# A 3x3 convolution: one half-image store cut into a 112-partition piece and four 4-partition pieces

## The chip, the cores and the metric

The kernel runs on one core of a Trainium2 chip. The metric is the device time of one execution in microseconds (us), the median of several runs. A core has five engines that run their own instruction queues side by side: TensorE (PE, matrix products), VectorE (DVE), ScalarE (ACT), GpSimd (POOL) and SyncE (SP, which here only issues transfers and waits). Transfers between the chip's main memory (HBM) and the core's own memory (SBUF, 128 partitions) are done by 16 DMA engines. A transfer is cut into packets, each of which is handled by one DMA engine; here a packet is one partition's contiguous row. When all DMA engines that take part have reported, the transfer has landed.

## What is computed

A 3x3 convolution with padding 1 of 16 images of 64 channels and 64x64 pixels to 128 channels. Nine tenths of the weights are zero, but the kernel treats them as dense.

```python
for b in range(batch):            # 16
    for co in range(c_out):       # 128
        for ci in range(c_in):    # 64
            for kh in range(k):
                for kw in range(k):
                    output[b, co] += weight[co, ci, kh, kw] * x_pad[b, ci, kh:kh+h, kw:kw+w]
```

Input and output are float32; an output image is 128 channels by 4096 pixels, 2 MB, and the whole output is 33.55 MB.

## The kernel before

Images go in pairs: eight pairs, p = 0 to 7. The 64 channels of the pair's two images lie side by side on the 128 partitions of a tile `xs[p]` in bfloat16. POOL issues the loads of all pairs at the start (L63, L67), with the conversion on the way; SP issues the weights (L60) and half of the first pair (L62). The weights are converted, transposed on PE, and summed and subtracted into five sets of taps (L103 to L118).

For each pair, four blocks of 16 rows are worked off in order (the loop at L175). Nearly all go through `twos` (L151): POOL adds neighbouring rows of x (L154), PE multiplies the sums (L157) and ACT copies that product to SBUF (L161); PE then multiplies the even and the odd rows' remaining terms, and DVE adds the copied product and writes the result into the pair's output tile `o[n]` (L168), n = 0 and 1 for the two images. The very first block uses `direct` (L144) instead. All products come from L135. The scheduler is manual: the order of instructions on each engine is the order in which the code is written.

An output tile `o` has 128 partitions (the output channels) of 64 x 64 float32, 16 KB each. The pool of these tiles has seven buffers (L47); the first tile of it holds the half pair that SP loads (L61), the other sixteen are the output images. When a pair is done, SP issues one store for each of its two images (L188): 128 partitions of 16 KB each. For the last pair SP issues two stores per image, of 32 rows each, so 8 KB per partition (L185). SP's queue holds, in order, the two loads, 14 stores of L188, four stores of L185, and the waits for their landing at the end of the program (L214).

The stores of p = 0 to 7 are issued as soon as DVE has written the pair. Those of the sixth pair (p = 5) are the eleventh and twelfth of L188's stores.

Of the kernel before, what the change touches and what calls it, by code (L numbers as in the profile page):

```python
# [27 lines left out]
def kernel(  # L28
# [6 lines left out]
    nc = tc.nc  # L35

    B, C_IN, H, W = x.shape
    C_OUT, _, KH, KW = weight.shape
    assert (B, C_IN, H, W) == (16, 64, 64, 64) and (C_OUT, KH, KW) == (128, 3, 3)
    NP = B // 2  # L40
# [103 lines left out]
    def direct(p, o, r0, rows):  # L144
        ps = product(
            [(xs[p], G1, r0, 1), (xs[p], G0, r0 - 1, 1), (xs[p], G2, r0 + 1, 1)], rows
        )
        nc.scalar.copy(out=o[0][:, r0 : r0 + rows, :], in_=ps[0])  # L148
        nc.vector.tensor_copy(out=o[1][:, r0 : r0 + rows, :], in_=ps[1])  # L149

    def twos(p, o, r0):  # L151
        t0 = r0 // 2
        s = s_pool.tile([128, 8, W], BF16, name="s")
        nc.gpsimd.tensor_tensor(  # L154
            out=s, in0=xs[p][:, r0 : r0 + 16 : 2, :], in1=xs[p][:, r0 + 1 : r0 + 16 : 2, :], op=ADD
        )
        shared = product([(s, G1, 0, 1)], 8)  # L157
        pc = []
        for n in range(2):
            c = p_pool.tile([128, 8, W], FP32, name="pc")  # L160
            nc.scalar.copy(out=c, in_=shared[n])  # L161
            pc.append(c)
        even = [(xs[p], G21, r0 + 1, 2), (xs[p], G0, r0 - 1, 2)]
        odd = [(xs[p], G01, r0, 2), (xs[p], G2, r0 + 2, 2)]
        for first, terms in ((r0, even), (r0 + 1, odd)):
            ps = product(terms, 8)
            for n in range(2):
                nc.vector.tensor_tensor(  # L168
                    out=o[n][:, first : r0 + 16 : 2, :], in0=ps[n], in1=pc[n], op=ADD
                )  # L170

    for p in range(NP):
        o = [o_pool.tile([C_OUT, H, W], FP32, name="o") for _ in range(2)]
        last = p == NP - 1
        for blk in range(4):  # L175
            r0 = 16 * blk
            if BLOCKS[p][blk] == "T":
                twos(p, o, r0)
            else:
                for r, rows in ((r0, 8), (r0 + 8, 8)):  # L180
                    direct(p, o, r, rows)
            if last and blk % 2 == 1:
                for n in range(2):
                    rows = slice(r0 - 16, r0 + 16)
                    nc.sync.dma_start(out=out[2 * p + n][:, rows, :], in_=o[n][:, rows, :])  # L185
        if not last:
            for n in range(2):
                nc.sync.dma_start(out=out[2 * p + n], in_=o[n])  # L188


# [28 lines left out]
```

## Time and profile before

| what | value |
|---|---|
| time, median of 6 runs | 127.7 us (127.58 to 127.92) |
| time of the profiled execution | 127.75 us |
| its span, from the first to the last instruction | 125.9 us |
| PE busy | 108.9 us, 86% of the span |
| DVE busy | 82.3 us, 65% |
| ACT, POOL busy | 39.0 and 40.8 us |
| granted TensorE clock, mean | 0.95 |
| HBM read and written | 17.07 and 33.55 MB, 402 GB/s over the span |
| stores of a whole image (L188) | 14, median 18.5 us from issue to landing |
| stores of half an image (L185) | 4, median 10.9 us |

The times of the groups of instructions come from one profiled execution; the median comes from runs beside it. In the profile the 16 DMA engines are shown together: a share of 1.00 means that all of them were at work all the time. The packet records of the trace give each packet's start, duration and size, but not the number of the DMA engine; the landing records give the time of each of the sixteen reports of a transfer. Where the text speaks of one engine's packets, they were put together from these records: each packet of an engine begins a few nanoseconds before the end of the one before it.

### The profile page before, as it was taken

The page shows a single profiled execution, that of the slowest core. Times are in us where ns is not written, and L with a number is a line of the kernel's source. Part 1 is how long each engine was busy: PE and PEld are TensorE (multiplying, and loading weights), DVE is VectorE, ACT ScalarE, POOL GpSimd, SP SyncE. Part 2 cuts the span into 40 slices and gives each one's busy share as a digit, 9 for nine tenths or more (in the row PEclk, how much of TensorE's full clock was granted, in tenths as well). Part 3 has the DMA queues.
Part 4 walks back from the last instruction along what each step waited for, and adds up shares of the span by engine and source line. Part 5 has one row for each costly group of instructions (what it writes and reads, how often), then busy time and mean ns, then how long its engine had stood idle before and what let it go on. Part 6 is the DMA issues. An engine that isn't in the chain of part 4 may idle for free.

```text
span 125.9 us, 2486 instructions
## 1 busy us (share of the span) xinstructions
PE 108.9 (86%) x1002; PEld 59.1 (47%) x1002; DVE 82.3 (65%) x135; ACT 39.0 (31%) x71; POOL 40.8 (32%) x45
## 2 busy tenths in 40 slices
PE   6569999999999999999999999999999999960000
PEld 6334555555555555555555555555555555520000
DVE  0352477877787778777787778777877787771000
ACT  4541533333333333333333333333333333320000
POOL 6937333333333333333333333333333320000000
PEclk9977999999999999999999999999999999999555
DMA  4999999999999999999999999999999999999980
GB/s 115 352 223 221 213 219 213 208 182 338 302 315 333 333 299 333 320 312 346 427 437 422 416 432 443 432 424 411 427 443 427 437 417 416 432 414 414 424 346 18
DMA packets 4044, 42.93 MB, mean 341 GB/s; under 512 B 448, under 2 KB 448, under 8 KB 704
## 3 DMA queue, kind: packets, MB, share of 16 engines
q1 hardware_dynamic: 2880, 34.90, 66.0%
q0 software_dynamic: 1152, 7.86, 30.8%
q8 instruction: 8, 0.13, 0.4%
q14 instruction: 4, 0.03, 0.1%
HBM read 17.07 MB, written 33.55 MB: 402 GB/s over the span
## 4 chain that ended last, share of the span: by engine, by line
PE 82%; DMA 4%; DVE 1%; issue 1%; DVEq 0%; SPq 0%
PE ps L135 82%; DMA o<-in_x_dram 4%; DVE o L168 1%; DVEq L214 0%; DVE x L87 0%; SPq L60 0%; DVEq L168 0%
## 5 line engine op out<-in xcount | busy, mean ns | idle before, releaser
L168 DVE TENSOR_TENSOR o<-ps,pc 128x512 f32<-128x512 f32 x124 | 77.8, 686 | 22.1 <-PE ps L135 19.8
L135 PE MATMUL ps<-x,wT 64*128 64x504 bf16 (+3 forms) x780 | 90.5, 379 | 2.0 <-DVE x L87 2.0
L135 PEld LDWEIGHTS <-wT 64*128 64x128 bf16 x966 | 55.8, 95 | 50.9 <-issue 3.6
L154 POOL TENSOR_TENSOR s<-x 128x512 bf16<-128x512 bf16 x31 | 35.7, 1152 | 59.6 <-PE ps L135 43.2
L161 ACT COPY pc<-ps 128x512 f32<-128x512 f32 x62 | 33.3, 589 | 64.0 <-issue 61.8
L135 PE MATMUL ps<-s,wT 64*128 64x512 bf16 (+1 forms) x186 | 25.7, 377 | 0.0
L74 PE MATMUL ps<-idle_rhs 128*128 128x128 bf16 x27 | 3.1, 313 | 1.0 <-DVE idle_rhs L71 1.0
L149 DVE COPY o<-ps 128x512 f32<-128x512 f32 x2 | 1.4, 692 | 3.7 <-PE ps L135 3.7
L67 POOL DMA_DIRECT2D x<-in_x_dram x7 | 3.7, 556 | 0.0
L74 PEld LDWEIGHTS <-idle_rhs 128*128 128x128 bf16 x27 | 2.8, 148 | 1.0 <-DVE idle_rhs L71 1.0
L91 DVE CAST w_bf<-w_sb 128x192 bf16<-128x192 f32 (+1 forms) x4 | 1.1, 347 | 2.9 <-DMA w_sb<-in_weight_dram 2.9
L148 ACT COPY o<-ps 128x512 f32<-128x512 f32 x2 | 1.2, 586 | 4.1 <-PE ps L135 4.1
L87 ACT CAST x<-o 128x576 bf16<-128x576 f32 (+1 forms) x2 | 1.5, 802 | 0.9 <-DMA o<-in_x_dram 0.9
L87 DVE CAST x<-o 128x576 bf16<-128x576 f32 x1 | 0.5, 460 | 1.8 <-DMA o<-in_x_dram 1.8
L91 ACT ACT_TABLE_LOAD x1 | 1.3, 1283 | 0.7 <-PEq L203 0.7
L91 ACT CAST w_bf<-w_sb 128x64 bf16<-128x64 f32 (+1 forms) x2 | 0.7, 415 | 1.8 <-DMA w_sb<-in_weight_dram 1.8
L97 PE MATMUL ps<-ident,w_bf 128*128 128x128 bf16 x9 | 0.9, 222 | 0.4 <-DVE w_bf L91 0.4
L101 DVE TENSOR_TENSOR wT<-ps,wT 128x384 bf16<-128x384 f32 x2 | 1.0, 548 | 0.0
L63 POOL DMA_DIRECT2D x<-in_x_dram x1 | 0.7, 696 | 0.8 <-POOLq L203 0.8
L97 PEld LDWEIGHTS <-w_bf 128*128 128x128 bf16 x9 | 0.5, 97 | 0.9 <-DVE w_bf L91 0.9
L71 DVE MEMSET idle_rhs<- 128x64 uint32 x1 | 0.1, 112 | 0.8 <-PEq L203 0.8
L112 DVE CAST wT<-ps 128x384 bf16<-128x384 f32 x1 | 0.6, 551 | 0.0
(8 smaller groups left out, 1.9 us busy)
## 6 DMA issues: line engine op xcount, KB each, us to landing
out_dram<-o SPq DMA_DIRECT2D x14, 2048.0 KB, 18.5
x<-in_x_dram POOLq DMA_DIRECT2D x7, 1024.0 KB, 27.3
out_dram<-o SPq DMA_DIRECT2D x4, 1024.0 KB, 10.9
o<-in_x_dram SPq DMA_DIRECT2D x1, 1024.0 KB, 5.6
x<-in_x_dram POOLq DMA_DIRECT2D x1, 512.0 KB, 7.7
w_sb<-in_weight_dram SPq DMA_DIRECT2D x1, 288.0 KB, 3.1
```

The lines of the kernel that those rows point to most:

```text
L67: nc.gpsimd.dma_start(out=xs[p], in_=pair(p))
L74: nc.tensor.matmul(idle_ps, idle_rhs, idle_rhs, start=True, stop=True)
L87: copy(out=xs[0][:, a:b, :], in_=x_head[:, a:b, :])
L91: copy(out=w_bf4[:, g, a:b, :], in_=w_v[:, k : k + b - a, :])
L97: nc.tensor.matmul(wps[:, j, :], src, ident, start=True, stop=True)
L101: nc.vector.tensor_tensor(out=wT[:, g], in0=wps, in1=wT[:, G1], op=SUB)
L135: nc.tensor.matmul(ps[n][:, lo:hi, c_lo:c_hi], tap(g, kw, n), src[q, a:b:step, c_lo + kw - 1 : c_hi + kw - 1], start=(i == 0), stop=(i == ...
L148: nc.scalar.copy(out=o[0][:, r0 : r0 + rows, :], in_=ps[0])
L149: nc.vector.tensor_copy(out=o[1][:, r0 : r0 + rows, :], in_=ps[1])
L154: nc.gpsimd.tensor_tensor(out=s, in0=xs[p][:, r0 : r0 + 16 : 2, :], in1=xs[p][:, r0 + 1 : r0 + 16 : 2, :], op=ADD)
L161: nc.scalar.copy(out=c, in_=shared[n])
L168: nc.vector.tensor_tensor(out=o[n][:, first : r0 + 16 : 2, :], in0=ps[n], in1=pc[n], op=ADD)
```

## The change

The store of image 0 of the sixth pair (p = NP - 3 = 5, n = 0) is issued in six pieces. Its first 32 rows are one store of 128 partitions with 8 KB each. Its last 32 rows are one store of partitions 0 to 111, and four stores of 4 partitions each (112 to 115, 116 to 119, 120 to 123, 124 to 127), again with 8 KB per partition. All other stores are as before, and so is every instruction of the other engines. By the change's own description, the 112 partitions give every DMA engine seven packets where it had eight, and each store of 4 partitions gives one packet to each of the DMA engines 0 to 3, so that these carry three packets of 8 KB more and all others one less.

```diff
         if not last:
             for n in range(2):
-                nc.sync.dma_start(out=out[2 * p + n], in_=o[n])
+                pieces = [(0, 128, 0, H)]
+                if (p, n) == (NP - 3, 0):
+
+                    pieces = [(0, 128, 0, H // 2), (0, 112, H // 2, H)]
+                    pieces += [(c, c + 4, H // 2, H) for c in range(112, 128, 4)]
+                for c0, c1, a, b in pieces:
+                    nc.sync.dma_start(
+                        out=out[2 * p + n][c0:c1, a:b, :], in_=o[n][c0:c1, a:b, :]
+                    )
```

## The prediction

> **What bounds the kernel now.** I read the page's slices first, then the chain that ended last, the waits of SP, a table of windows over the end, and last the trace's packet and landing records (start and duration of each DMA packet; time at which each of a store's sixteen engines reported). The slices:
>
> ```profile
> PE   6569999999999999999999999999999999960000
> ...
> DMA  4999999999999999999999999999999999999980
> ```
>
> PE is full until about 112 us. The DMA engines are full too, and go on alone for the last four slices. The chain of work, in order of time, follows only engines, and ends with DVE:
>
> ```profile
> 7.31 103.77 PE ps L135 x954
> ...
> 111.75 0.68 DVE o L168
> 112.43 0.60 DVEq L214
> 113.03 0.60 DVE o L168
> ```
>
> The span is 125.9 us, so 12.3 us lie behind that last addition. The waits of SP's queue say what they are: at the program's end (L214) SP waits for the last stores.
>
> ```profile
> SPq L188 <- DVE o L168: 94.1, 14, 21.8
> SPq L185 <- DVE o L168: 10.5, 4, 5.3
> SPq L214 <- DMA out_dram<-o: 9.8, 4, 2.6
> ```
>
> The table of windows shows how the transfers end (the last two columns are the share of the 16 DMA engines that is busy, and GB/s):
>
> ```profile
> 62.00:90.00 28.00, 28.00 (x266) 15.04 (x264) 21.90 (x36) 9.43 (x18) 10.24 (x9) 1.00 1.01 427
> ...
> 120.00:121.00 1.00, 0.00 (x0) 0.00 (x0) 0.00 (x0) 0.00 (x0) 0.00 (x0) 0.50 0.99 418
> 121.00:122.00 1.00, 0.00 (x0) 0.00 (x0) 0.00 (x0) 0.00 (x0) 0.00 (x0) 0.50 0.76 320
> 122.00:123.00 1.00, 0.00 (x0) 0.00 (x0) 0.00 (x0) 0.00 (x0) 0.00 (x0) 0.50 0.39 164
> 123.00:124.00 1.00, 0.00 (x0) 0.00 (x0) 0.00 (x0) 0.00 (x0) 0.00 (x0) 0.50 0.10 41
> ```
>
> From 62 us on the stores have a backlog and all engines stay full; at the end they run out one by one between 121 and 124.3 us. The last store's landing records are 121.46, 121.60, 121.79, 122.13, 122.16, 122.24, 122.39, 122.81, 122.96, 122.98, 123.01, 123.25, 123.32, 123.39, 123.79 and **124.74**. The latest engine sets the end: 1.14 us later the span is over. So the time is that of the slowest DMA engine, and a packet moved from one engine to another counts at full price from the changed store on.
>
> **The change, part by part.** The sum is made against the profiled execution: span 125.9 us, 1.85 us around it, 127.75 us. The median of six is 127.7.
>
> *Packets.* Packets of 16 KB (a full store's row) last 611 ns in 1190 of the 1279 records from 62 to 111 us, and overlap by 4: 607 each. A full store is eight of them per engine and a 6 ns report, 4.862 us, which is the distance of landings. Packets of 8 KB (half a row) last 309 ns, 305.7 each; the last four stores land 2.452 us apart. The changed store then takes on engines 4 to 15 2.452 + 7 x 0.3057 + 0.006 = 4.598 us, that is **0.264 us less**. On engines 0 to 3 four packets with reports of their own are added, 4 x 0.312 = 1.247, so 5.845 us, **0.983 us more**.
>
> *At the end.* If the latest engine is not among 0 to 3, it lands at 124.74 - 0.264 = 124.48. Engines 0 to 3 stay below that if they landed by 123.49 before, as 14 of 16 did. The records have no engine numbers. Four engines drawn from the other fifteen have their latest at four fifths, the 12th: 123.25, which becomes 124.23. Counting alone gives 127.75 - 0.26 = 127.49.
>
> The latest engine is a special one: its 16 KB packets last 634 to 662 ns while the compute engines run, and those of the rest 611. The Trainium skill ("DMA: Bandwidth & Descriptors", Latency and other measured facts) says that engines 7 and 15 are usually the slower ones. This trace has one slow engine and no numbers; by that rule it lies outside 0 to 3, and counting gives -0.26 and not +0.98 us.
>
> *Who reads what.* In each store of before, the same 128 rows are dealt to the 16 engines in the same way, and one engine's packets do not lengthen another's: 611 ns nearly everywhere. 112 rows in sevens can't keep that deal. The seven packets of an engine fall on rows that in the full stores belong to its neighbours, which are at work at the same time; the four pieces give engines 0 to 3 sixteen rows whose usual engines are, at that moment, reading others of their own rows. Eleven packets of engines 0 to 3, and up to seven of every other, may share a way into SBUF. No row of this case shows two engines on one way. From below the price is nothing (a gain is excluded: an engine that reads its own rows is at its best, 611). From above, the nearest rows are load packets between 25.5 and 28 us, when the first stores come in beside the loads: 0.8 to 1.25 us and once 1.42, against 0.625 alone, so about a doubling. The window's rate fell with it:
>
> ```profile
> 25.50:28.00 2.50, 2.50 (x27) 1.28 (x24) 1.77 (x4) 1.07 (x2) 1.15 (x1) 1.00 0.96 138
> ```
>
> I take a doubling where an engine surely meets another one (the four pieces, whose rows' own engines never pause) and half of the seven: 7.5 x 0.306 = 2.29 us on engines 0 to 3, 3.5 x 0.306 = 1.07 us on the others. Ends: 0 and 11 x 0.306 = 3.36 us. Engines 0 to 3 then land at 123.25 + 0.983 + 2.29 = 126.52, the slow engine at 124.48 + 1.07 = 125.55. The end moves by 126.52 - 124.74 = 1.78: 127.75 + 1.78 = **129.5 us**. With all eleven doubled, at the 14th landing: 123.39 + 0.983 + 3.36 = 127.73, 130.7 us.
>
> Why I take it although the loads speak against it: from 10 to 22 us an engine needs 606 ns for a load packet that reads 16 KB but writes only 8 KB to SBUF, so the engine's own rate is the limit there, and the way into SBUF may have room. But 16 stores' streams of 27.0 GB/s without a trace of scatter look like sixteen separate ways. The Trainium skill ("SBUF — State Buffer", Door 1: The DMA port swizzle) speaks against this change: eight partitions hang on one port, and four partitions alone reach 27.6 GB/s. By it a port's bytes do not change when another engine fetches them, nothing can be gained, and two engines on a port get half each, an estimate of 0.61 us a packet; no run here shows it.
>
> *Issuing.* SP issues six DMAs where it issued one. Two issues take 0.93 us:
>
> ```profile
> 87.45 0.93 SPq L188 DMA_DIRECT2D out_dram<-o  x2
> ```
>
> At 0.60 each, the store queued behind them on SP (the pair's second image) is issued at 91.05 and not 88.05. The first engine reports the changed store at 97.06 and only then needs the next: 6 us of cover, so nothing. If a piece took 1.05 us, as the slowest issue (L185) does, 93.3 would still do. Nobody else is on SP until pair 6 at 100.25. The o tile of this store is the twelfth of 17 in seven buffers, so no later tile waits for it. PE, DVE, ACT and POOL have the same instructions in the same order.
>
> **The rivals.**
> - *No sharing* (the other side): counting alone holds, 127.49 us, 0.21% faster. For it: the load packets above. Against it: the even 611. It decides as long as engines 0 to 3 lose less than 124.74 - 124.23 = 0.5 us over eleven packets, 46 ns each, and the slow engine less than 0.26 us over seven, 38 ns each.
> - *The slow engine is one of 0 to 3*, without sharing: 124.74 + 0.98, 128.7 us. One in four by blind drawing; against it, in the rush of 25.5 to 28 us this engine's packets lengthen later than those of at least six others, so it is hardly one of the first four to be served.
> - *The pieces don't spread*: all sixteen packets on one engine, 16 x 0.312 - 0.264 = +4.7 us; at a middle landing of 122.9 that is 127.6, so 130.6 us.
>
> **How the numbers follow.** Sharing at a price that shows: 0.52, forecast 129.5, its own range 128.0 to 130.8. No sharing: 0.36; the expected gain of 0.21% lies at the limit of 0.2%, which is about what a measurement of this kernel can tell from no change, so I split it 0.23 faster and 0.13 the same. Light sharing that eats just the gain: 0.04, the same. Slow engine among 0 to 3: 0.05. No spread: 0.03. Faster 0.23, same 0.17, slower 0.60. The range reaches from 127.4 (counting, less a tenth) to 131.0 (all eleven doubled, and some scatter); sharing by more than two engines at once, left out, has about one in ten.
>
> **What would show it.** In the packet records after about 92 us: 112 + 16 packets of 8 KB with 309 ns say no sharing, with 400 to 700 sharing. Sharing would also press the rate below 420 GB/s for some microseconds in the windows between 92 and 100. At the end, the window of 123 to 124 us is emptier if counting holds and busier, with landings past 125, if not. A PE or DVE wait that is new would prove me wrong on the cover, and a landing of the pair's second image that is late by itself on the issuing. The forecast is wrong if two engines can read one group of rows at full speed.

## The result, and the profile after

The changed kernel takes **128.6 us** (median of 21 runs, 127.61 to 129.51); the kernel before, beside it, 127.72 us (42 runs, 127.28 to 128.8). The ratio is 1.0057, with a 95% interval of 1.0037 to 1.0077: slower, by 0.7 us and not by 1.8. Ratios leave out runs more than 1.5% above the fastest of their kernel, and need not be those of the medians beside them. The 21 runs fall in two groups with nothing between 127.90 and 128.29: 8 runs at 127.61 to 127.90, which is the time before, and 13 at 128.29 to 129.51. The profiled execution belongs to the upper group: 129.27 us, span 127.5.

The first two fences are the busy rows and the chain of the changed kernel. PE's chain starts 0.5 us later than before and takes 1.2 us longer (105.0 us against 103.8), and the last addition is at 114.72 us.

```profile
PE   6659999999999999999999999999999999970000
...
DMA  4999999999999999999999999999999999999950
```

```profile
7.77 105.01 PE ps L135 x954
...
113.44 0.68 DVE o L168
114.13 0.60 DVEq L222
114.72 0.60 DVE o L168
```

So the last addition is 1.7 us later than in the profile of before. That is no part of the loss: 12.2 us of transfers still lie behind it, and the same long time came again (129.45 and 128.84 us, below) in executions in which the first store was issued earlier than here. SP's waits (us in total, times, longest) show one line that is new, the last:

```profile
SPq L194 <- DVE o L168: 91.0, 15, 23.5
SPq L185 <- DVE o L168: 9.9, 4, 4.8
SPq L222 <- DMA out_dram<-o: 9.7, 1, 9.7
SPq L194 <- DMA out_dram<-o: 2.7, 1, 2.7
```

The new wait is of SP for a landing before it may issue a store. It ended at 94.5 us, and the next store's data were only there at 101.95: it costs nothing.

The windows answer to those of before (the last two columns are the share of the 16 DMA engines that is busy, and GB/s):

```profile
94.00:97.00 3.00, 3.00 (x32) 1.49 (x30) 2.27 (x5) 1.07 (x2) 1.15 (x1) 1.00 1.00 421
97.00:99.60 2.60, 2.60 (x28) 1.31 (x26) 2.31 (x4) 0.89 (x2) 0.79 (x1) 1.00 1.07 425
...
122.00:123.00 1.00, 0.00 (x0) 0.00 (x0) 0.00 (x0) 0.00 (x0) 0.00 (x0) 0.50 0.75 311
123.00:124.00 1.00, 0.00 (x0) 0.00 (x0) 0.00 (x0) 0.00 (x0) 0.00 (x0) 0.50 0.16 66
124.00:125.00 1.00, 0.00 (x0) 0.00 (x0) 0.00 (x0) 0.00 (x0) 0.00 (x0) 0.50 0.08 33
125.00:126.00 1.00, 0.00 (x0) 0.00 (x0) 0.00 (x0) 0.00 (x0) 0.00 (x0) 0.50 0.04 16
```

Two things are to be seen. While the changed store is under way (94 to 99.6 us), the sum of all engines hardly changes: 421 and 425 GB/s, where before had 421 and 429 in the same windows. The rows of before:

```profile
94.00:97.00 3.00, 3.00 (x31) 1.57 (x29) 2.27 (x5) 0.85 (x2) 1.03 (x1) 1.00 0.98 421
97.00:99.60 2.60, 2.60 (x28) 1.46 (x26) 1.87 (x5) 1.07 (x2) 1.15 (x1) 1.00 1.02 429
...
124.00:125.00 1.00, 0.00 (x0) 0.00 (x0) 0.00 (x0) 0.00 (x0) 0.00 (x0) 0.50 0.00 0
```

And the end has a thin tail: from 124 us on, a share of 0.08 and 0.04 is one engine of sixteen, alone for almost two microseconds. By the packet records, the last report of a DMA engine is at 125.71 us, the one before it at 124.47; before the change they were at 124.28 and 123.39. (The landing records, which the prediction used, give each report some 0.4 us later.) The end is 1.43 us later, the span 1.6, the time 1.52.

**Which engine, and where it lost the time.** The last one is the same special engine as before, the one whose 16 KB packets take 634 to 662 ns while the compute engines run. Below it is called the slow engine. Its packets can be followed one by one, since it never idles. The store before the changed one ends on it at 93.912 us before and at 93.974 after, the same. Then, from the packet records of the changed kernel:

```
slow engine   eight packets of the first half   318 to 342 ns each, report at 96.56
              seven packets of the 112-piece    508 632 628 612 309 487 854 ns, report at 100.63
others        report of the first half -> report of the 112-piece: 2.147 us on each of the fifteen
engines 0-3   four pieces each: 309 309 309 309 on three of them, 380 571 511 433 on the fourth
```

The landing records of the 112-piece say the same without any following of packets: fifteen landings from 96.78 to 98.43, and one at 101.03. Seven packets at the slow engine's own pace are 2.3 us; it took 4.07, so it lost 1.8 us there, saved one packet of 0.3, and ended 1.43 later.

### The profile page after: what moved, and what is told of

It is laid out like the page before. It is cut to its first block, busy times and chain, and to the rows that moved or that the text cites. A ratio compares the mean times of both kernels' runs of the same rounds, so it can differ in the third digit from the quotient of the medians.

```text
span 127.5 us, 2492 instructions
## 1 busy us (share of the span) xinstructions
PE 110.5 (87%) x1002; PEld 56.9 (45%) x1002; DVE 82.3 (65%) x135; ACT 38.9 (31%) x71; POOL 40.7 (32%) x45
## 4 chain that ended last, share of the span: by engine, by line
PE 82%; DMA 5%; DVE 1%; issue 1%; DVEq 0%; SPq 0%
PE ps L135 82%; DMA o<-in_x_dram 5%; DVE o L168 1%; DVEq L222 0%; DVE x L87 0%; SPq L60 0%; DVEq L168 0%
## 5 line engine op out<-in xcount | busy, mean ns | idle before, releaser
L135 PE MATMUL ps<-x,wT 64*128 64x504 bf16 (+3 forms) x780 | 91.5, 382 | 2.3 <-DVE x L87 2.3
L135 PEld LDWEIGHTS <-wT 64*128 64x128 bf16 x966 | 53.3, 96 | 55.0 <-issue 5.7
L110 ACT CAST wT<-ps 128x384 bf16<-128x384 f32 x1 | 0.5, 478 | 0.4 <-PE ps L97 0.4
```

The costliest lines, as they stand in the source:

```text
L135: nc.tensor.matmul(ps[n][:, lo:hi, c_lo:c_hi], tap(g, kw, n), src[q, a:b:step, c_lo + kw - 1 : c_hi + kw - 1], start=(i == 0), stop=(i == ...
```

## The experiments

e2 to e5 were timed beside one set of runs of the kernel before, e1 and e6 to e8 beside a second, e9 to e11 beside a third and e12 beside a fourth. Short diffs are against the changed kernel. Theories: the four pieces cost it (as forecast); the deal of 112 rows in sevens costs it; the earlier issue of the first half costs it (SP issued it at 82.69 us, before the rest of the image was done); or the loss is scatter of single executions.

**e2: the deal of 112 without the pieces.** The last 16 partitions go as one store, one packet for each engine, so every engine carries what it did before.

```diff
-pieces = [(0, 128, 0, H // 2), (0, 112, H // 2, H)]
-pieces += [(c, c + 4, H // 2, H) for c in range(112, 128, 4)]
+pieces = [(0, 128, 0, H // 2), (0, 112, H // 2, H), (112, 128, H // 2, H)]
```

> The half image is cut into 112 and 16 partitions: every DMA engine should get seven packets and then one, so the counts are those of before, and only the deal of the rows differs. Theory A (the deal of 112 rows in sevens makes the slow engine's packets double, about 1.8 us on it): 1.006 to 1.014 of before, the slow engine's seven packets 500 to 850 ns. Theory B (the four pieces of 4 partitions disturb): 1.000, packets of 309 to 340 ns. Theory C (the loss comes from compute that starts 1.7 us later in some executions, not from the change): scatter as in before, 1.000.

Measured: 128.91 us (127.48 to 129.64, 12 runs) against 127.72; ratio 1.006, interval 1.0028 to 1.0092. It costs as much as the whole change, with no piece of 4 partitions and no rebalancing. So neither the pieces nor the three packets more on engines 0 to 3 are needed for a loss of this size. Its profiled execution was one of the short ones (127.99 us); there only the last packet of the seven was long on the slow engine (336, 319, 342, 324, 347, 324, **774**), and one packet of 847 ns fell on another. None of its longer executions left a trace, so that they lose in the same way is likely and not shown.

**e3: the pieces without the deal of 112.** Rows 60 to 63 of partitions 0 to 111 of this image are left out.

```diff
-pieces = [(0, 128, 0, H // 2), (0, 112, H // 2, H)]
+pieces = [(0, 128, 0, H // 2), (0, 128, H // 2, H - 4)]
 pieces += [(c, c + 4, H // 2, H) for c in range(112, 128, 4)]
```

> The half image is stored with all 128 partitions but 28 of its 32 rows, and the four pieces follow as in the change (rows 60 to 63 of partitions 0 to 111 are left out, so this part of the output is missing). Each engine carries 7/8 of a half store in the usual deal, and engines 0 to 3 four packets more. Theory A: no loss, counting alone holds, -0.26 us, 0.998. Theory B: as the change, 1.003 to 1.008, and packets of 16 KB on some engines of 700 to 1200 ns beside the pieces. Theory C: 1.000.

Measured: 132.14 us (131.95 to 132.31, 4 runs), ratio 1.0332, 1.0289 to 1.0375. This says nothing of the pieces. They write rows again that the store before them writes, so SP had to wait for that store to land, and the queues ran dry. SP's waits and two windows show it:

```profile
SPq L193 <- DMA out_dram<-o: 11.2, 1, 11.2
```

```profile
97.00:99.60 2.60, 2.60 (x28) 1.31 (x25) 1.87 (x4) 1.07 (x2) 1.15 (x1) 1.00 0.17 72
99.60:102.00 2.40, 2.40 (x27) 1.28 (x24) 1.82 (x4) 1.07 (x2) 1.15 (x1) 1.00 0.20 41
```

A share of 0.17 and 0.20 for 5 us is the loss. What can be used is that the 7 KB packets of the 128-partition store beside it took 272 ns each (slow engine 276 to 301) with none lengthened.

**e4 and e8: the changed kernel again,** without an edit, to see whether the same engine loses again.

> The changed kernel once more, for a second trace. Theory A: the slow engine's seven packets are lengthened again whenever the time is above 128.2 us, and are near 320 ns when it is near 127.7. Theory C: the time goes with the moment of the first store's issue (23.5 or 25.2 us), and the slow engine's packets are alike in both.

> The changed kernel a third time, for its trace. The time is near 127.7 or near 129; in the first case the slow engine's seven packets take 310 to 350 ns, in the second several of them 500 to 850.

Measured: e4 129.22 us (129.07 to 129.45, 4 runs; 1.0105, 1.0063 to 1.0148), profiled 129.45; e8 a single run of 128.84. Both traces show the slow engine's seven packets lengthened again, from the second or third on: 336, 581, 621, 618, 309, 495, 855 and 339, 326, 519, 640, 309, 572, 840. Its landing of the 112-piece is at 101.25 where the others end at 98.66, and at 100.65 with 98.68. e4's windows have the same one-engine tail:

```profile
124.00:125.00 1.00, 0.00 (x0) 0.00 (x0) 0.00 (x0) 0.00 (x0) 0.00 (x0) 0.50 0.08 33
125.00:126.00 1.00, 0.00 (x0) 0.00 (x0) 0.00 (x0) 0.00 (x0) 0.00 (x0) 0.50 0.04 16
```

The pieces of engines 0 to 3 were mostly at 309 ns again; the exceptions (501, 388, 564 in e4; 369, 631, 627, 493, 982 in e8) fell on two engines in each trace. In e4 the seventh packet of the 112-piece was long on three other engines too (534, 516, 444). Scatter that would choose any engine does not explain three traces with the same one.

**e1: two halves of 128 partitions.**

```diff
-pieces = [(0, 128, 0, H // 2), (0, 112, H // 2, H)]
-pieces += [(c, c + 4, H // 2, H) for c in range(112, 128, 4)]
+pieces = [(0, 128, 0, H // 2), (0, 128, H // 2, H)]
```

> The same store in two half stores of 128 partitions each, so the usual deal and the usual counts, with two DMAs for one. Theory A (the deal of 112 rows costs): 1.000, no packet of the slow engine above 345 ns. Theory D (any earlier issue of half a store, 82 instead of 87 us, disturbs the queues): 1.003 to 1.008.

Measured: 127.62 us (127.22 to 128.1, 12 runs) against 127.67, ratio 0.9992, 0.9971 to 1.0013. All sixteen packets of the slow engine took 314 to 342 ns, and no packet of another engine was lengthened. So splitting, issuing early and 8 KB packets cost nothing that can be measured; the deal does.

**e7: two halves of the partitions,** four packets per engine and store; another deal than that of 128, with even counts.

```diff
-pieces = [(0, 128, 0, H // 2), (0, 112, H // 2, H)]
-pieces += [(c, c + 4, H // 2, H) for c in range(112, 128, 4)]
+pieces = [(0, 128, 0, H // 2), (0, 64, H // 2, H), (64, 128, H // 2, H)]
```

> The second half image in two transfers of 64 partitions: four packets and four packets on each engine, so the counts of before, but engines read rows that in the usual deal belong to others. Theory A in its wide form (every row read by another than its usual engine is read at half speed when both are at work): up to eight packets doubled, 0.3 to 2.4 us on the end, 1.003 to 1.019. Theory A in its narrow form (only sevens, or only certain rows, do harm): 1.000.

Measured: 128.0 us (127.62 to 129.71, 12 runs), ratio 1.0018, 0.9995 to 1.0041, which can't be told from none. In the profiled execution (127.77 us) the slow engine was undisturbed (311 to 349 ns); one other engine had 462, 768 and 880 ns (1.18 us lost in all) and two more had one long packet each (734 and 459), and these do not set the end. Another deal lengthens packets here too, but on engines that have time.

**e5: 120 + 8,** another uneven deal, which was to give a gain: fifteen engines carry eight packets each of the first piece, eight of these one more, and the sixteenth none.

```diff
-pieces = [(0, 128, 0, H // 2), (0, 112, H // 2, H)]
-pieces += [(c, c + 4, H // 2, H) for c in range(112, 128, 4)]
+pieces = [(0, 128, 0, H // 2), (0, 120, H // 2, H), (120, 128, H // 2, H)]
```

> The half image is cut into 120 and 8 partitions. If a transfer of 120 partitions goes over 15 engines with eight packets each, and one of 8 over the first eight, then the last engine gets none. If the slow engine is the last one, it is 2.45 us earlier at the end, the others decide, and the time falls by 0.6 to 0.9 us (0.993 to 0.995) if rows in eights do no harm; with harm as in theory A on the lagging engine alone, the same gain, since that engine has no packet there. If the slow engine is another, it keeps eight packets or gets a ninth: 1.000 to 1.003, or 1.006 to 1.014 with theory A.

Measured: 128.27 us (127.9 to 128.91, 12 runs), ratio 1.0041, 1.0017 to 1.0065: slower, where a gain was hoped for. Here an ordinary engine had 438, 598, 628, 645, 482, 639, 638 and 852 ns, 2.4 us lost, and the end has two late reports, at 124.82 and 125.04, of which the slow engine, whose ninth packet took 831 ns, is not the later. More packets were long here on other engines (452 to 979 ns). So the harm is no property of the slow engine. That the deal decides on which engine it falls is an inference.

**e6 and e10: which engine is it?** The trace has no engine numbers, but a store of n partitions (n up to 16) shows n packets on n engines. The last two rows of five earlier stores are stored for the first few partitions only, as marks, and left out for the others (about 0.3 MB, some 0.7 us of transfers at the 430 GB/s of this stage).

```diff
+marks = {(2, 1): 12, (3, 0): 4, (3, 1): 6, (4, 0): 7, (4, 1): 8}     # e6
+marks = {(2, 1): 14, (3, 0): 5, (3, 1): 2, (4, 0): 10, (4, 1): 12}   # e10
+if (p, n) in marks:
+    pieces = [(0, 128, 0, H - 2), (0, marks[p, n], H - 2, H)]
```

> The changed kernel, and in five earlier stores the last two rows are cut off and stored for the first 12, 4, 6, 7 and 8 partitions alone (for the other partitions they are left out). A transfer of k partitions up to 16 should take the first k engines, one packet of 512 bytes each, so the marks tell which engines are 0 to 3, 4 and 5, 6, 7, 8 to 11. It shows which number the slow engine has: 7 or 15 by the rule cited in the prediction, outside 0 to 3 by the prediction itself. Theory A expects the lengthened packets of 8 KB on the slow engine again, 500 to 850 ns, where the time is over 128.2 us.

> The changed kernel with marks of 14, 5, 2, 10 and 12 partitions in the last two rows of the same five earlier stores (for the other partitions these rows are left out). The first marks put the slow engine at 4 or 5; a mark of 5 tells which. If it is 4, its rows in sevens are 28 to 34 and the engine that is lengthened beside it is 7, which reads rows 28 to 31 in its full stores, so it carries the marks of 10, 12 and 14 but not those of 2 and 5. If the time is near 127.5 the slow engine's sevens are near 330 ns, if near 129 several of them are 500 to 850.

Measured: one run each, 127.5 and 126.73 us (their times are with rows left out). The marks nest: the four engines of the 4-partition pieces are those of the mark of 4. The slow engine carries the marks of 12, 10, 8, 7, 6 and 5, and not those of 4 and 2. So it is the fifth in the order in which engines are filled: not one of 0 to 3, and **number 4** if they are counted from 0. In both traces it was undisturbed (324 to 342 and 314 to 352 ns), and the lengthened packets (471, 772, 344, 406; 381, 645, 361, 621, 484, 607, 834) were on others. e10's time plus the 0.7 us that it leaves out is 127.4, near the 127.49 of counting alone; e6's is 128.2 and is not. In e6 the slow engine is done at 123.42, 0.86 us before its time in the kernel before, and not the last. Another engine reports at 124.21 and sets the end: the one that fetches 16 KB of instructions at 114.0 us, between two of its own packets (385, 931 for the fetch, 704). Every trace has such a fetch at 111 to 117 us. In the kernel before (340, 949, 691) and in the changed one, the engine that has it is the second last to report, at 123.39 and 124.47. So a slow engine that gets earlier may no longer be the last one, and a sum that counts the packets of the stores alone leaves that other engine out.

**e9: the same cut two pairs earlier,** where the engines still have some 45 us to the end.

```diff
-if (p, n) == (NP - 3, 0):
+if (p, n) == (3, 0):
```

> The same cut, but of image 0 of the fourth pair (p = 3) and not of the sixth. Theory A with lag (the deal in sevens hurts the engine that is behind while the others are already in the next full store; the slow engine falls back by 0.3 us with every store and is not yet the last one there): the lengthened packets fall on engines that do not set the end, the slow engine's stay at 310 to 350 ns, and counting alone holds: -0.26 us, 0.998. Theory A without lag (the slow engine is hurt wherever the cut stands): 1.006 to 1.010 as in the change.

Measured: 127.84 us (127.47 to 131.45, 12 runs), ratio 1.0001, 0.9979 to 1.0022. There the lengthened packets are found too (660, 458, 1114, 554, and a neighbour's 1418), but the slow engine kept about 328 ns. Neither a loss nor a gain can be measured. SP's new wait is larger there:

```profile
SPq L193 <- DMA out_dram<-o: 15.1, 5, 4.6
```

Issuing more stores makes SP wait more often for one of the stores before; still nothing ran dry (a DMA share of 0.98 or more from 62 to 90 us).

**e11 and e12: the same packets on other rows.** The 112 partitions are 16 to 127, and the pieces come from 0 to 15. Counts and engines are those of the change; only which rows an engine reads is different.

```diff
-pieces = [(0, 128, 0, H // 2), (0, 112, H // 2, H)]
-pieces += [(c, c + 4, H // 2, H) for c in range(112, 128, 4)]
+pieces = [(0, 128, 0, H // 2), (16, 128, H // 2, H)]
+pieces += [(c, c + 4, H // 2, H) for c in range(0, 16, 4)]
```

> The half image is cut into partitions 16 to 127 in sevens and four pieces of partitions 0 to 15: counts as in the change, but each engine's seven rows move by 16. If the slow engine is hurt because of the rows that it reads there (those of one neighbour that is reading the same rows in its full store), other rows may be free or not: 0.998 if they are free, 1.006 to 1.010 if any foreign rows hurt. If the rows do not matter, 1.006 to 1.010.

> The kernel with the 112-partition group moved to partitions 16 to 127 and the four small pieces taken from partitions 0 to 15, once more, for a profile of an ordinary execution. By the theory that the loss is the lengthened packets of the slow engine (number 4): its seven packets stay at 314 to 350 ns each, its report of that transfer comes about 2.3 us after the one before, and the time is 0.998 to 1.000 of the time before. By the rival that the rebalancing as such costs the 0.6%, wherever the group lies: 1.004 to 1.008, with the seven packets of that engine lengthened to some 4 us as with partitions 0 to 111.

Measured: 127.73 us (127.22 to 130.39, 12 runs; ratio 0.999, 0.9966 to 1.0015) and 127.68 us (127.2 to 129.36, 12 runs; 1.0005, 0.9972 to 1.0037). e11's profile shows its longest execution. PE's chain began at 11.37 us there (7.31 before), so the stores came late and the DMA engines were not full all the time, as the 4 in its slices shows; the last report is not the slow engine's. e12 is the same kernel once more, for an ordinary execution.

```profile
DMA  4999999999999999999999999999999949999990
```

In both traces the slow engine's seven packets are free: 314 to 347 ns, and 336, 328, 324, 333, 338, 333, 324. Others are not: e12 has 702, 598, 585, 632, 999, 607 and 849 ns between 95 and 99 us, on engines that don't set the end. The windows of e12 have no tail behind 124 us:

```profile
120.00:121.00 1.00, 0.00 (x0) 0.00 (x0) 0.00 (x0) 0.00 (x0) 0.00 (x0) 0.50 0.99 418
121.00:122.00 1.00, 0.00 (x0) 0.00 (x0) 0.00 (x0) 0.00 (x0) 0.00 (x0) 0.50 0.85 360
122.00:123.00 1.00, 0.00 (x0) 0.00 (x0) 0.00 (x0) 0.00 (x0) 0.00 (x0) 0.50 0.41 172
123.00:124.00 1.00, 0.00 (x0) 0.00 (x0) 0.00 (x0) 0.00 (x0) 0.00 (x0) 0.50 0.10 41
```

The last four reports are at 123.32, 123.50, 123.53 and 123.64 (before: 122.99, 123.04, 123.39, 124.28): the slow engine no longer stands out, and this execution took 127.2 us. Of its 0.64 us, 0.30 were there before the changed store (its first half began on the slow engine at 93.61 instead of 93.91); the other 0.34 are about the packet that it no longer has. Over all runs the expected 0.26 us can't be seen: both intervals hold 0.998 and 1. Four of e12's twelve runs took 128.4 to 129.36, so in some executions something is late here too; whether it is a lengthened packet their lack of a trace leaves open. Counted over all runs, 18 of 26 of the changed kernel (with e4 and e8) took more than 128.25 us, 6 of 24 of the shifted one (e11 and e12), and 9 of 128 of the kernel before. So the shift takes away most of the long executions, and it is not shown that it takes away all.

The slow engine's seven packets in all traces with seven per engine, beside the profiled time. The second column is its report of the store before the changed one, where the execution already stands early or late:

| kernel | report of the store before | seven packets, first start to report | profiled time, us |
|---|---|---|---|
| changed kernel | 93.97 us | 4.07 us | 129.27 |
| e4, the same | 94.48 | 3.84 | 129.45 |
| e8, the same | 94.17 | 3.55 | 128.84 |
| e2, 112 + 16 | 93.96 | 2.75 | 127.99 |
| e6 and e10, marks (rows left out) | 93.14 and 93.25 | 2.30 and 2.28 | 127.5 and 126.73 |
| e12, shifted | 93.61 | 2.30 | 127.2 |
| e11, shifted, compute late | 93.91 | 2.28 | 130.39 |
| e9, cut at p = 3 | 73.29 | 2.30 | 127.64 |

In the first four rows the two columns add up to the end: the slow engine's last report (125.71, 125.90, 125.27, 124.74) lies 27.5 to 27.7 us behind their sum, in e2 after taking off its one packet of the last 16 partitions (373 ns). e11 is the one long execution whose seven packets are free; its length has the other cause named above.

No version is faster than the kernel before by more than its interval.

## Why the prediction was wrong in size

The direction was right, the forecast of 129.5 us was not: the time rose by 0.7 us by the ratio and by 0.9 by the medians, not by 1.8. The sign is in part luck: the engines that were to decide, 0 to 3, did not, and the slow engine, put below them at 125.55, landed at 126.17.

- *What bounds the kernel*: right. The end is the last report of the slowest DMA engine, and the shift of that report (1.43 us) is the shift of the time (1.52 us) but for 0.1.
- *Packets*: right. Seven undisturbed packets and their report took 2.147 us on fifteen engines (7 x 0.3057 + 0.006 = 2.146), a piece 0.312. The 0.264 us less on the slow engine is real: where its packets stayed free, the changed store took it 4.89 to 4.90 us (e6, e10, e12), against 5.16 in the kernel before. That the whole time follows was too simple. The engine with the instruction fetch stood 0.89 us behind in the profile of before, and it set the end of e6; the prediction has no term for it.
- *At the end*: right that the latest engine is not among 0 to 3; the marks say so (not 4, but 5). Engines 0 to 3 with their 0.98 us more did not set the end in any trace of the changed kernel. (The latest of four drawn from fifteen stands nearer the 13th place, 123.32, than the 12th; it would have moved the sum by 0.07 us.) The page's rule did not hold here: the Trainium skill ("DMA: Bandwidth & Descriptors", Latency and other measured facts) names 7 and 15 as the usually slower ones, the marks say 4.
- **Who reads what: this step failed.** It priced every piece at double (with half of the seven, 2.29 us on engines 0 to 3) and the others at 1.07 us, so that engines 0 to 3 decide at 126.52. Measured on engines 0 to 3 in the changed kernel's profile: nothing on three of them, 0.66 us on the fourth (380, 571, 511, 433); 12 of 16 pieces ran at 309 ns with all the other engines at work. On the others: nothing in the seven packets of the 11 ordinary ones (two engines lost 0.77 and 0.34 us in the first packets of their next store), and 1.8 us on the slow one, where 1.07 was put. What was right in it is that rows dealt out of their usual order can lengthen packets to 400 to 700 ns, and more. What was wrong is that it happens to all alike, and in every execution. It falls on a few engines, and it costs time when it falls on the one that is last anyway, or when it makes an engine the last one (e5). In this profile the sum is then 124.28 - 0.26 + 1.8 = 125.8, against 125.71 measured.
- *Rivals.* The lower group of 8 runs (median 127.73) is not at the 127.49 of "no sharing", but at the time before. The chances treated sharing and no sharing as a question with one answer; the kernel gives both, in about 13 and 8 of 21 executions. That the lower group are executions in which the slow engine is spared is inferred from e6, e10 and e12; none of the three traces of the changed kernel itself was of that group.
- *Issuing*: right, the second image's landing is not late by itself. That the first half would be issued early, at 82.69 us, was not foreseen; e1 shows that it costs nothing measurable. A wait was added that the text had not foreseen, 2.7 us, in the cover.
- *What would show it*: the windows of 92 to 100 us were to fall below 420 GB/s with sharing. Where packets were lengthened, from 96.6 us on, they did not (421 and 425; the 414 of 92 to 94 us lies ahead of that): one engine of 16 at half pace is 3% for 2 us. Only the packet and landing records show it.

**How the deal can do it.** The Trainium skill ("DMA: Bandwidth & Descriptors", The descriptor swizzle) states that with 128 partitions engine 4 carries 16 to 19 and 48 to 51, and engine 7 carries 28 to 31 and 60 to 63. It doesn't state the deal of 112; if each engine takes seven rows in a run, engine 4 reads 28 to 34, the first four of which are engine 7's, and with the shift by 16 it reads 44 to 50. That would fit: in the changed kernel's trace an engine outside 0 to 3 had 713, 1222 and 648 ns from the second packet of its next store on, the first two of them while the slow engine read its first four rows. But no record names rows, the last packets (487, 854) have no such partner that can be seen, and by "SBUF — State Buffer" (Door 1), which gives a port about 27 GB/s for its eight partitions, the pieces should have shared as well; 12 of 16 did not.

So it is shown that a deal other than that of 128 partitions lengthens packets (e2, e5, e7, against e1), that the slow engine's lengthened packets account for the three long executions of the changed kernel that were traced (the table), and that with the rows shifted it has none in both traces (e11, e12). What is shared, why the last of seven is the longest (774 to 855 ns), and why some executions are spared, stays open.

## What to carry to other kernels

When all DMA engines are full to the end, the time is that of the engine that ends last: read the landing records of the last stores before and after, and follow that engine's packets, since the windows hide a loss of 1.8 us on one of sixteen. Moving packets between DMA engines by cutting stores along the partitions also changes which rows each engine reads, and that can cost more than a packet: cut along the free dimension where possible (e1 costs nothing measurable), and test any other cut on several profiles. Where the runs of a kernel fall in two groups, one profile shows one of them; forecast the share of the groups, and not only a price.

## What the runs showed of the hardware

- Rows 112 to 127, read four at a time by engines 0 to 3, were mostly read at full pace: in the changed kernel's profile 12 of 16 pieces took 309 ns per 8 KB (26.5 GB/s) in the middle of a full stream.
- The slow engine is the fifth in the order of filling (634 to 662 ns against 611 per 16 KB while compute runs); in the last 12 us of before's stores, when nothing is computed any more, hardly a packet of it was over 312 ns, so there it is as fast as the others.
- An instruction fetch of 16 KB took 0.88 to 0.97 us on one DMA engine (all traces, from 96 us on), and the 16 KB packet beside it at 97 to 103 us 0.97 to 1.02 us instead of 0.61, about 1.3 us in all. The engine that has the fetch at 111 to 117 us loses about as much there; it set the end in e6 and e11.
- SP waits, before it issues a store, for the landing of the store eight issues earlier: 2.7 us once in the changed kernel, 15.1 us in five waits in e9.
